# The norm's row: four broadcast matmuls of 128 columns in place of two of 256

## The chip, the cores and the metric

The kernel runs on one core of a Trainium2 chip. The metric is the device time of one execution in microseconds (us), the median of several runs. Each run of the profiler gives one more execution, with its own time.

## The reference, cut to what matters

A decoder trunk of two layers over 256 tokens of width 1024, in float32. Each layer is half an FFN, a mixer (attention and pooling in the even layer, spatial gating in the odd one) and another half FFN. Each of these six parts normalises its input first:

```python
def _rmsnorm(x, g):
    xf = x.astype(jnp.float32)
    y = xf * lax.rsqrt(jnp.mean(xf * xf, axis=-1, keepdims=True) + EPS)
    return (y * g.astype(jnp.float32)).astype(x.dtype)
...
    for layer in range(DEPTH):
        h = h + 0.5 * _swiglu(_rmsnorm(h, ffn_norm[layer, 0]), ffn_w_gate[layer, 0],
                              ffn_w_up[layer, 0], ffn_w_down[layer, 0])
        hn = _rmsnorm(h, mix_norm[layer])
        ...
```

The gain g is applied to the input of a projection; the factor rsqrt(...), one number for each token, is applied to the projection's output.

## The kernel before

The residual stream lies transposed in the chip's memory: 128 features on the partitions, eight such blocks, 256 tokens along the columns. Every weight arrives by DMA on SyncE's queue in chunks of up to 128 x 1024, is rounded by ScalarE into a high part (L169) and by VectorE into a low part (L177), and so each product of a weight and an activation is made of a few products of the type fp32r: mm2 (L216, L217) in the FFNs, with 256 and 512 columns, and mm3 (L210 to L212) in the mixers, with 256 to 512 columns. Products that aren't split have the type F32: the means of squares (L284, one column), the attention's values (L859 to L861, 64 columns), the mixing of the odd layer (L973, 128 columns), and the transposes (L563, L566, L793, L851, L874).

The order of the instructions on each engine is written out by hand (L107): it is the order of the calls in the program. The banks of the accumulator memory come in two sets of four, acc and rot.

The norm is worked in three steps. While the previous part ends, norm_hi, norm_lo and norm_sq (L264 to L279) make the scaled input x and the sums of squares. norm_sum (L281) multiplies them by a column of 1/1024 on TensorE, adds EPS on VectorE, takes the power -1/2 on GpSimd (L250), splits the result into a high and a low part, and writes, on GpSimd, each part times the identity into the tile diag (L295 to L298): four pieces of 128 x 128, high part first, left token half first. norm_row (L300) then multiplies a matrix of ones (ones_r, fp32r) by the low and the high diagonal. That puts each token's factor on all 128 partitions, as a row of 256 columns in the second half of a bank. ScalarE copies it to rb (L305), and in the FFNs VectorE copies half of it to rbh (L309).

norm_row runs six times, once in each part. In an FFN it is called in the second block of gate_up, before its third chunk, while norm_sum was called before its first one (L386); TensorE works on that block in between, and the epilogue of block 0, which multiplies by rb and rbh (L369, L371), follows at once. In the even mixer it stands behind the first two chunks of the pooling projection and right before the key and value products (L578, L623); in the odd mixer at the end of the first block of u (L994).

Of the kernel before, what the change touches and what calls it, by code (L numbers as in the profile page):

```python
# [16 lines left out]
P = 128  # L17
T = 256
TB = T // P
# [57 lines left out]
def trunk_kernel(  # L77
# [21 lines left out]
    nc = tc.nc  # L99
# [21 lines left out]
    def small(shape, tag, bufs=2):  # L121
        return spool.tile(shape, F32, tag=tag, name=nm(tag), bufs=bufs)
# [113 lines left out]
    ones_r = const.tile([P, P], F32R, name="ones_r")  # L236
# [19 lines left out]
    def norm_begin(gname, goff):  # L256
        s = Norm()
        s.gname, s.goff = gname, goff
        s.x = xpool.tile([P, KD, 2, T], F32R, tag="x", name=nm("x"), bufs=2)
        s.xl, s.xh = s.x[:, :, 0, :], s.x[:, :, 1, :]  # L260
        s.sum = None
        return s
# [36 lines left out]

    def norm_row(s, half=False):  # L300
        bc = s.bank[:, T : 2 * T]
        nc.tensor.matmul(bc, ones_r, s.dg[:, 1], start=True, stop=False, skip_group_check=True)
        nc.tensor.matmul(bc, ones_r, s.dg[:, 0], start=False, stop=True, skip_group_check=True)
        s.rb = small([P, T], "rb", bufs=2)
        nc.scalar.copy(s.rb, bc)  # L305
        if not half:
            return
        s.rbh = small([P, T], "rbh", bufs=2)
        nc.vector.tensor_scalar(s.rbh, bc, 0.5, None, op0=ALU.mult)  # L309
# [29 lines left out]
    def ffn(s, nxt_args, sets, first=False):  # L339
        with tc.tile_pool(name=nm("ffn"), bufs=2) as fp:  # L340
# [40 lines left out]
            def mid():  # L381
                norm_row(s, half=True)
                epilogue(0, gu0)
# [99 lines left out]
    def even_mixer(s, nxt_args):  # L483
        with tc.tile_pool(name="even", bufs=1) as ep:
# [91 lines left out]

            pool_in(0, turn_lat, 3)
            norm_row(s)  # L578
            advance(st["use"] + 4)
            nc.vector.tensor_mul(rqk, rqk, r1.unsqueeze(1).to_broadcast([P, 2, TB]))  # L580
# [329 lines left out]
    def odd_mixer(s, nxt_args):  # L910
        with tc.tile_pool(name="odd", bufs=1) as op:
# [78 lines left out]
            def gate_lo(c):  # L990
                cs = slice(2 * c, 2 * c + 2)
                nc.vector.tensor_sub(zl[:, cs, :], zs.pop(c), zh[:, cs, :].bitcast(F32))

            u_block(0, end=lambda: norm_row(s))  # L994
            for c in range(1, NG):
                def mid():
# [38 lines left out]
    s = norm_begin("ffn", 0)  # L1035
# [27 lines left out]
    s = ffn(s, ("mix", 0), (acc_bank, rot_bank), first=True)  # L1063
    s = even_mixer(s, ("ffn", KD))
    s = ffn(s, ("ffn", 2 * KD), (rot_bank, acc_bank))
    s = ffn(s, ("mix", KD), (acc_bank, rot_bank))
    s = odd_mixer(s, ("ffn", 3 * KD))
# [81 lines left out]
```

## Time and profile before

| | us |
|---|---|
| median of 3 runs | 909.33 (909.01 to 909.56) |
| profiled execution | 906.19 |
| its span, first to last instruction | 904.4 |
| TensorE's products (PE), busy | 894.2 |
| TensorE's weight loads (PEld), busy | 787.5 |
| VectorE (DVE), busy | 645.7 |
| ScalarE (ACT), busy | 496.1 |
| GpSimd (POOL), busy | 99.7 |

A product of TensorE has two records: the load of its 128 x 128 weights (PEld) and the product itself (PE). Their durations overlap, since both are pipelined and the ends of the products are modelled; what an instruction costs in a full stream is the time from its start to the start of the next one.

### The profile page before, as it was taken

To read this page: it belongs to the slowest core of one execution; us is meant where nothing else is said; L and a number is where in the kernel's file an instruction comes from. 1 tells how busy PE (TensorE), PEld (TensorE's weight loads), DVE (VectorE), ACT (ScalarE), POOL (GpSimd) and SP (SyncE) were. 2 spreads that over 40 slices of the span, in tenths; PEclk is the share of its full clock that TensorE was granted. 3 is DMA by queue.
4 is the path that set the end of the run, shared out by engine and by line. 5 is a ranking of instruction groups with operands and counts; after the bars stand their busy time and mean duration, and the time that the engine had idled before them with its cause. 6 is when DMAs were issued, how large, how long until landed. Compare 5 with 4: busy or idle time off the path is not lost.

```text
span 904.4 us, 13887 instructions
## 1 busy us (share of the span) xinstructions
PE 894.2 (99%) x5320; PEld 787.5 (87%) x5320; DVE 645.7 (71%) x973; ACT 496.1 (55%) x782; POOL 99.7 (11%) x130
## 2 busy tenths in 40 slices
PE   8999999999999999999999999999999999999998
PEld 6888888889898888888888888888899988888887
DVE  7787778658877877785558777756648668777652
ACT  7555554447575655564456555544545556555430
POOL 4200000016624000000030000000120220000000
PEclk9999999999999999999999999999999999999999
DMA  8565555635254555556644555575436455555750
GB/s 291 185 232 199 188 181 194 221 109 179 94 163 141 168 194 191 189 194 232 207 155 148 186 187 187 186 255 187 155 131 207 141 183 188 191 193 193 260 164 23
DMA packets 59281, 164.45 MB, mean 182 GB/s; under 512 B 5456, under 2 KB 7760, under 8 KB 59216
## 3 DMA queue, kind: packets, MB, share of 16 engines
q1 hardware_dynamic: 59216, 163.58, 54.0%
q8 instruction: 41, 0.67, 0.3%
q14 instruction: 24, 0.20, 0.1%
HBM read 162.51 MB, written 1.05 MB: 181 GB/s over the span
## 4 chain that ended last, share of the span: by engine, by line
PE 94%; DVE 2%; POOL 1%; issue 1%; ACT 1%; DMA 1%; SPq 0%; DVEq 0%; POOLq 0%
PE rot L217 27%; PE acc L217 26%; PE rot L216 13%; PE acc L216 13%; PE acc L211 3%; PE acc L210 3%; PE acc L212 2%; PE rot L210 1%; PE rot L211 1%; PE rot L212 1%; DMA raw<-w_gu 1%; PE rot L973 0%; POOL diag L297 0%; DVE wlo L182 0%; PE rot L821 0%
## 5 line engine op out<-in xcount | busy, mean ns | idle before, releaser
L177 DVE TENSOR_TENSOR wlo<-raw,whi 128x1024 fp32r<-128x1024 f32 (+2 forms) x298 | 353.1, 1228 | 76.3 <-ACT whi L169 76.2
L169 ACT CAST whi<-raw 128x1024 fp32r<-128x1024 f32 (+2 forms) x303 | 301.2, 1043 | 106.1 <-PE acc L217 39.8
L217 PE MATMUL acc<-x,whi 128*128 128x512 f32 x704 | 248.3, 397 | 0.0
L217 PE MATMUL rot<-x,whi 128*128 128x512 f32 x704 | 247.6, 396 | 0.0
L216 PE MATMUL acc<-x,wlo 128*128 128x256 f32 x704 | 197.7, 281 | 1.4 <-DVE wlo L182 1.4
L216 PE MATMUL rot<-x,wlo 128*128 128x256 f32 x704 | 196.6, 279 | 0.0
L217 PEld LDWEIGHTS acc<-x,whi 128*128 128x128 f32 x704 | 132.6, 188 | 31.3
L217 PEld LDWEIGHTS rot<-x,whi 128*128 128x128 f32 x704 | 132.2, 188 | 31.6
L216 PEld LDWEIGHTS acc<-x,wlo 128*128 128x128 f32 x704 | 133.1, 189 | 2.9 <-DVE wlo L182 2.9
L216 PEld LDWEIGHTS rot<-x,wlo 128*128 128x128 f32 x704 | 132.6, 188 | 0.0
L217 PE MATMUL rot<-pp,whi 128*128 128x512 f32 x352 | 123.4, 396 | 0.0
L217 PE MATMUL acc<-pp,whi 128*128 128x512 f32 x352 | 123.4, 396 | 0.0
L216 PE MATMUL acc<-pp,wlo 128*128 128x256 f32 x352 | 98.2, 279 | 0.0
L216 PE MATMUL rot<-pp,wlo 128*128 128x256 f32 x352 | 98.2, 279 | 0.0
L217 PEld LDWEIGHTS rot<-pp,whi 128*128 128x128 f32 x352 | 66.1, 188 | 15.9
L217 PEld LDWEIGHTS acc<-pp,whi 128*128 128x128 f32 x352 | 66.1, 188 | 15.9
L216 PEld LDWEIGHTS rot<-pp,wlo 128*128 128x128 f32 x352 | 66.3, 188 | 0.0
L216 PEld LDWEIGHTS acc<-pp,wlo 128*128 128x128 f32 x352 | 66.3, 188 | 0.0
L359 ACT COPY a<-rot 128x256 f32<-128x256 f32 x88 | 29.8, 373 | 55.5 <-PE rot L217 55.5
L359 ACT COPY a<-acc 128x256 f32<-128x256 f32 x88 | 29.8, 373 | 53.3 <-PE acc L217 53.3
L278 POOL TENSOR_TENSOR sqsum<-sq,sq 128x256 f32<-128x256 f32 x6 | 6.1, 1016 | 458.2 <-ACT sq L273 458.2
L361 DVE TENSOR_TENSOR gu<-rot,a 128x256 f32<-128x256 f32 x88 | 31.4, 419 | 34.1 <-ACT a L359 33.9
(246 smaller groups left out, 1037.4 us busy)
## 6 DMA issues: line engine op xcount, KB each, us to landing
raw<-w_gu SPq DMA_DIRECT2D x172, 512.0 KB, 4.6
raw<-w_down SPq DMA_DIRECT2D x88, 512.0 KB, 4.8
raw<-ew_out SPq DMA_DIRECT2D x8, 512.0 KB, 3.6
raw<-ow_v SPq DMA_DIRECT2D x8, 512.0 KB, 3.5
raw<-ow_u SPq DMA_DIRECT2D x8, 512.0 KB, 4.3
raw<-ow_out SPq DMA_DIRECT2D x8, 512.0 KB, 3.8
raw<-ew_p SPq DMA_DIRECT2D x4, 512.0 KB, 3.8
raw<-w_gu SPq DMA_DIRECT2D x7, 256.0 KB, 4.7
```

The lines of the kernel that those rows point to most:

```text
L169: nc.scalar.copy(hi[:, :n], r[:, :n])
L177: eng.tensor_sub(lo[:, :n], r[:, :n], hi[:, :n].bitcast(F32))
L210: nc.tensor.matmul(out, wl, xh, start=start, stop=False, skip_group_check=True)
L211: nc.tensor.matmul(out, wh, xl, start=False, stop=False, skip_group_check=True)
L212: nc.tensor.matmul(out, wh, xh, start=False, stop=stop, skip_group_check=True)
L216: nc.tensor.matmul(bank[:, 0:T], wl, x[:, 1, :], start=start, stop=False, skip_group_check=True)
L217: nc.tensor.matmul(bank, wh, x.rearrange("p s t -> p (s t)"), start=False, stop=stop, skip_group_check=True)
L278: nc.gpsimd.tensor_add(t, s.sum, sq)
L359: nc.scalar.copy(a[:, i, :], bank[:, 0:T])
L361: nc.vector.tensor_add(gu[:, i, :], bank[:, T:], a[:, i, :])
```

## The change

norm_row makes four products where it made two. The row of 256 columns is cut into two halves of 128 tokens; for each half the low diagonal and then the high one is multiplied by the same matrix of ones. Only the first of the four has `start=True`, and the high product of each half has `stop=True`. The sums are the same, and so is everything around.

```diff
     def norm_row(s, half=False):
         bc = s.bank[:, T : 2 * T]
-        nc.tensor.matmul(bc, ones_r, s.dg[:, 1], start=True, stop=False, skip_group_check=True)
-        nc.tensor.matmul(bc, ones_r, s.dg[:, 0], start=False, stop=True, skip_group_check=True)
+        for tb in range(TB):
+            ts = slice(tb * P, (tb + 1) * P)
+            nc.tensor.matmul(bc[:, ts], ones_r, s.dg[:, 1, ts], start=tb == 0, stop=False,
+                             skip_group_check=True)
+            nc.tensor.matmul(bc[:, ts], ones_r, s.dg[:, 0, ts], start=False, stop=True,
+                             skip_group_check=True)
         s.rb = small([P, T], "rb", bufs=2)
         nc.scalar.copy(s.rb, bc)
```

## Rows read from the trace of the kernel before

**Rows 1.** The busy time of the engines and the chain that ended last by engine (page), and the core's span with its mean granted TensorE clock.

```profile
PE 894.2 (99%) x5320; PEld 787.5 (87%) x5320; DVE 645.7 (71%) x973; ACT 496.1 (55%) x782; POOL 99.7 (11%) x130
PE 94%; DVE 2%; POOL 1%; issue 1%; ACT 1%; DMA 1%; SPq 0%; DVEq 0%; POOLq 0%
...
core 0: 904.4 us, clock 1.000
```

**Rows 2.** The two longest of ten lines of the waits of TensorE's products: who waited for whom, us in total, times, longest us.

```profile
PE acc L216 <- DVE wlo L182: 1.4, 4, 0.4
PE acc L302 <- POOL diag L297: 1.4, 1, 1.4
```

**Rows 3.** The instructions of L302: engine, operation, count, duration in ns (min/median/max), first and last start in us, shapes. PEldq is the queue of the weight loads.

```profile
L302 PEldq EVENT_SEMAPHORE  x5: 51/51/51, 211.5 to 730.8; - x5
L302 PE MATMUL acc<-diag,ones_r x4: 281/284/384, 27.8 to 672.3; 128*128 128x256 f32 x4
L302 PE MATMUL rot<-diag,ones_r x2: 279/280/280, 290.5 to 733.9; 128*128 128x256 f32 x2
```

**Rows 4.** The timeline of TensorE's products in the even mixer, the second and third FFN, the odd mixer and the fourth FFN: start in us, duration in us, engine, line, operation. L303's row, between the two of each pair, is left out.

```profile
213.59 0.28 PE L302 MATMUL acc<-diag,ones_r 128*128 128x256 f32 x1
...
213.83 0.39 PE L210 MATMUL acc<-whi,ckvl 128*128 128x512 f32 x1
...
290.51 0.28 PE L302 MATMUL rot<-diag,ones_r 128*128 128x256 f32 x1
...
290.74 0.28 PE L216 MATMUL acc<-x,wlo 128*128 128x256 f32 x1
...
474.46 0.28 PE L302 MATMUL acc<-diag,ones_r 128*128 128x256 f32 x1
...
474.69 0.28 PE L216 MATMUL rot<-x,wlo 128*128 128x256 f32 x1
...
672.30 0.28 PE L302 MATMUL acc<-diag,ones_r 128*128 128x256 f32 x1
...
672.54 0.28 PE L210 MATMUL acc<-x,wlo 128*128 128x256 f32 x1
...
733.89 0.28 PE L302 MATMUL rot<-diag,ones_r 128*128 128x256 f32 x1
...
734.13 0.29 PE L216 MATMUL acc<-x,wlo 128*128 128x256 f32 x1
```

**Rows 5.** The timeline of the first FFN around its norm_row, GpSimd (POOL), weight loads (PEld) and products (PE).

```profile
26.54 1.18 POOL L297 TENSOR_SCALAR diag<-cst_sb,r_lo 128x128 fp32r<-128x128 f32 x2
...
27.77 0.38 PE L302 MATMUL acc<-diag,ones_r 128*128 128x256 f32 x1 [1.41 <-POOL diag L297]
...
28.00 0.19 PEld L216 LDWEIGHTS rot<-x,wlo 128*128 128x128 f32 x1
...
28.00 0.28 PE L303 MATMUL acc<-diag,ones_r 128*128 128x256 f32 x1
28.11 0.28 PE L216 MATMUL rot<-x,wlo 128*128 128x256 f32 x1
```

**Rows 6.** The timeline of TensorE's products in the even mixer, where products of 512 columns are followed by products of 384.

```profile
216.37 0.39 PE L212 MATMUL acc<-whi,ckvh 128*128 128x512 f32 x1
216.60 0.33 PE L210 MATMUL rot<-whi,cql 128*128 128x384 f32 x1
216.77 0.34 PE L211 MATMUL rot<-wlo,cqh 128*128 128x384 f32 x1
```

**Rows 7.** The timeline of TensorE's products of few columns: the odd mixer (L973, 128 columns), the start of the fourth FFN (L284, one column), the even mixer (L860 and L861, 64 columns). A row with x8 stands for eight instructions in a row.

```profile
688.70 1.06 PE L973 MATMUL rot<-wt,v_sb 128*128 128x128 f32 x8
689.51 0.36 PE L210 MATMUL acc<-x,wlo 128*128 128x256 f32 x1
...
727.82 0.58 PE L284 MATMUL rot<-cmean,sqsum 128*128 128x1 f32 x4
728.26 0.36 PE L216 MATMUL acc<-x,wlo 128*128 128x256 f32 x1
...
242.14 0.39 PE L860 MATMUL rot<-v_sb,pT 128*128 128x64 f32 x2
242.36 0.39 PE L861 MATMUL rot<-v_sb,pT 128*128 128x64 f32 x2
242.58 0.28 PE L851 MATMUL rot<-cst_sb,sm 128*128 128x128 f32 x1
```

**Rows 8.** The weight loads grouped by line and shape: count, busy us, mean ns of one, idle before. The two remaining loads of L302 and of L303 write into a bank named rot.

```profile
L284 PEld LDWEIGHTS acc<-cmean,sqsum 128*128 128x128 f32 x16 | 2.2, 190 | 1.1 <-issue 1.0
L860 PEld LDWEIGHTS rot<-v_sb,pT 128*128 128x128 f32 x16 | 2.4, 192 | 0.0
...
L303 PEld LDWEIGHTS acc<-diag,ones_r 128*128 128x128 f32 x4 | 0.8, 190 | 0.0
L302 PEld LDWEIGHTS acc<-diag,ones_r 128*128 128x128 f32 x4 | 0.8, 189 | 1.8 <-POOL diag L297 1.7
...
L566 PEld LDWEIGHTS rot<-cst_sb,lat 128*128 128x128 f32 x4 | 0.5, 140 | 0.0
```

**Rows 9.** The instructions of L265 in the first 20 us and of L216 in the first 14 us: count, duration in ns (min/median/max), first and last start in us.

```profile
L265 ACT ACTIVATE x<-par_h x8: 492/496/508, 3.1 to 14.0; 128x256 fp32r<-128x256 f32 x8
...
L216 PE MATMUL acc<-x,wlo x20: 274/280/562, 4.7 to 13.6; 128*128 128x256 f32 x20
```

## The prediction, made before the changed kernel ran

> **What bounds the kernel now.** I read the page first. TensorE's products are recorded as busy for 99% of the span and its weight loads for 87%; no other engine passes 71%. The chain that ended last is 94% TensorE [rows 1]. So time added to TensorE's stream is time added to the run, unless it falls where TensorE waits anyway. The list of its waits is short: ten lines, of which the two longest are 1.4 us each; the second of these is a wait of the lines that change, for the diagonal at L302, once [rows 2]. The granted clock was 1.000 over the whole span [rows 1], the higher of the two levels (2.4 GHz), so rows from different stages can be compared.
>
> Next, the two lines themselves. norm_row runs six times; L302 stands there six times, each a product of 256 columns [rows 3], and L303 likewise; each has a weight load of its own, though all load the same ones_r [rows 8]. The start times in the timeline tell more than the durations, since the records overlap: from the start of L302 to the start of the product behind L303 it is 0.24 us in the even mixer, 0.23 in the second FFN, 0.23 in the third, 0.24 in the odd mixer, 0.24 in the fourth FFN [rows 4], 1.18 us for the five. The first FFN is different: there L302 comes after the wait, and from 27.77 to 28.11 the pair takes 0.34 us, 0.23 of it the first step [rows 5]. I count that as about 0.12 of start-up after a wait and two ordinary steps of 0.11.
>
> **What the change does to TensorE.** Twelve products of 256 columns become 24 of 128. The streamed columns stay the same (6 x 512); the weight loads double, from 12 to 24. What a 128-column product of this type costs is not in the trace: none with fp32r operands is narrower than 256 columns. I bound it.
>
> Lower end, streaming alone. A 512-column fp32r product takes 0.23 us from start to start and a 384-column one 0.17 [rows 6], a 256-column one 0.12 (half of the 0.24 of the pair) [rows 4]. That is 0.45 ns a column, proportional, so 128 columns would be 0.058 us, and four of them 0.232: as much as the pair takes now.
>
> Upper end, the price of a plain F32 product. In mix_block (L973) four F32 products of 128 columns are eight instructions, and the eight steps to the next product's start take 0.81 us, 0.10 each [rows 7]. With the 0.11 of the next paragraph, two of them make 0.222 us a product.
>
> Between them stands the weight load. Each product needs one, and the trace shows what a step is when the columns are too few to hide it. The mean products have a single column (L284): four instructions between 727.82 and 728.26, 0.11 us each. The value products have 64 columns (L860, L861): four between 242.14 and 242.58, again 0.11 [rows 7]. One column and 64 columns cost the same step, so the step there isn't streaming; it is the load. The fp32r loads of L302 and L303 have the same recorded duration as those (189 and 190 ns beside 190 to 192), while the loads of the transposes at L566 are shorter, 140 ns [rows 8]. The timeline of the first norm shows how a load lies: the load of the next product starts when the product before it starts (load of L216 at 28.00 beside L303 at 28.00) [rows 5]. A 256-column product of 0.12 us just covers a load of 0.11; one of 0.058 doesn't, and the load becomes the step. I take 0.111 us a product, the row nearest in kind (same load, fewer columns than 256), and keep 0.058 and 0.222 as the ends.
>
> The Trainium skill speaks for a price between the lower end and mine: "TensorE: Matmul & The Clock Gate", section "Back-to-back issue gap", puts a sustained stream of load and product pairs at about 81 ns for 128 columns. By that, as an estimate, the change would cost 0.4 us instead of my sum. No 128-column pair of this trace goes that fast: the steps at L973 are 0.10 [rows 7], so the trace does not agree.
>
> **The sum.** Five norms in a full stream: 4 x 0.111 = 0.444 each, 2.22 for the five, against 1.18 now: +1.04 us. All of it lies on the path, since TensorE doesn't wait there.
>
> The first norm waits for the diagonal, written in four pieces by GpSimd in the order high part left, high right, low left, low right. The two low pieces run from 26.54 to 27.72, so about 0.6 us each [rows 5]. Now L302 needs both low pieces. After the change the first two products need only the left pieces, about 0.6 us earlier; they fit into the wait, and two are left for after it: 0.12 + 2 x 0.111 = 0.34 us, as now, so nothing. That holds if a wait is set by the piece that is read. It is so elsewhere: the products of the first FFN read the tile x from 4.7 us on, while its last piece is written at 14.0 [rows 9]. If all four products waited for the last piece, it would be +0.22.
>
> Other engines: ScalarE's copy at L305 and then VectorE's L309 come 0.2 us later in each norm. Behind that copy ScalarE has the epilogue and the casts of the next weights (L169) queued, and TensorE needs both later; but none of the ten lines of its waits names L169, L177, L305, L309 or the epilogue, the longest being the split of the first chunks at L182 [rows 2], so the delay stays inside their slack. If that cover were gone, each norm would cost up to the same 0.2 us once more. In the even mixer the key and value products come right behind the pair [rows 4]; they and what hangs on them shift by the same 0.2 us, which is in the sum. No DMA and no GpSimd step is moved. A wait added in the middle of the four could show as a 51 ns semaphore instruction on TensorE's queue, as five of the six L302 have one [rows 3]; those before L302 cost no visible time, so I take nothing, and six times 0.051 = 0.31 us as the other end.
>
> Total +1.04 us: 906.19 us of the profiled execution becomes 907.23. The median of the runs, 909.33, stands 3.14 us above that execution; the same addition gives 910.37, rounded 910.4. With the two unkind ends (+0.22, +0.31) it is 910.9.
>
> **The rivals.**
> A narrow product is charged as plain F32 (slower). The fp32r rate would hold only for wide products, and at 128 columns each would cost 0.222 us. Five norms: 4 x 0.222 = 0.888, less 0.236 now, times five: +3.26. The first: 0.12 + 2 x 0.222 = 0.56 against 0.34, +0.22. Together +3.48, so 912.8. It decides as soon as a step is over about 0.15 us. For it: no fp32r product under 256 columns is there to deny it. Against: from 512 to 256 columns the cost falls in proportion, with no sign of a second price.
>
> The loads hide after all (no change). If a load of ones_r were as short as those of the transposes (some 50 ns less), or if a second load of the same weights cost nothing, streaming would set the step: 5 x 0.232 - 1.18 = -0.02, and in the first norm 0.12 + 2 x 0.058 = 0.24 against 0.34, -0.10. That gives 909.2. Against it: the records of these very loads are 189 ns, as long as those of the 0.11 us steps, and L303's load isn't shorter than L302's [rows 8]. The skill's 81 ns, named above, would land between, at an estimated 909.8.
>
> **How the numbers follow.** A measurement of this kernel tells about 0.2% from no change, 1.82 us: from 907.5 to 911.15 counts as the same. Load-bound step, 910.4 (up to 910.9): 0.70. F32 price, 912.8: 0.17. Hidden loads, 909.2: 0.10. Anything else, a shift of other waits in either direction: 0.03. So the same 0.80, slower 0.19, faster 0.01; a gain of 1.8 us has no place, as the only wait the change can shorten is 1.4 us long. The range goes from the hidden loads with the spread of the runs, 909.0, to the F32 price, 912.8.
>
> **What would show it.** In the profile of the changed kernel: 24 products of 128 columns and 24 loads under norm_row; from the first of the four to the product behind them 0.44 us in five norms (0.23 if loads hide, 0.89 at the F32 price); in the first norm two products at about 27.2 and two after 27.7, and the product behind them at 28.1. It would be wrong if the four were 0.44 us and the span didn't grow, which would mean that a later wait gave it back, or if the span grew by far more than the four steps, which would mean that something waits for the late row.

## The result and the profile after

The changed kernel takes 900.83 us (900.25 to 901.08, five runs). The ratio to the kernel before is 0.9913, 95% interval 0.9896 to 0.993: 0.9% faster, where no change was forecast and a gain of over 0.2% had been given a chance of 0.01. The five runs of the kernel before in that comparison stand at 909.01, 909.33, 909.47 and 909.56, and one at 906.12.

TensorE's products fill 99% of the span, as before; there are twelve products and twelve loads more. The first two lines of the page that answer to [rows 1]:

```profile
PE 888.1 (99%) x5332; PEld 789.8 (88%) x5332; DVE 644.9 (72%) x973; ACT 496.1 (55%) x782; POOL 99.6 (11%) x130
PE 94%; DVE 2%; POOL 1%; issue 1%; DMA 0%; ACT 0%; SPq 0%; DVEq 0%; POOLq 0%
```

L304 is the low product of the changed norm_row, L306 the high one. The instructions of L304 (answering to [rows 3]):

```profile
L304 PEldq EVENT_SEMAPHORE  x5: 51/51/51, 207.9 to 724.7; - x5
L304 PEld LDWEIGHTS acc<-diag,ones_r x8: 186/192/192, 26.8 to 666.1; 128*128 128x128 f32 x8
L304 PE MATMUL acc<-diag,ones_r x8: 223/275/328, 26.8 to 666.1; 128*128 128x128 f32 x8
L304 PE MATMUL rot<-diag,ones_r x4: 222/247/272, 286.9 to 728.0; 128*128 128x128 f32 x4
```

Twelve of L304 and twelve of L306, each of 128 columns, each with a load of some 190 ns: the change does what it says. The timeline of the products around norm_row in the second FFN (start and duration in us), to be held against [rows 4]:

```profile
286.64 0.39 PE L217 MATMUL acc<-x,whi 128*128 128x512 f32 x1
286.87 0.22 PE L304 MATMUL rot<-diag,ones_r 128*128 128x128 f32 x1
286.93 0.27 PE L306 MATMUL rot<-diag,ones_r 128*128 128x128 f32 x1
287.04 0.27 PE L304 MATMUL rot<-diag,ones_r 128*128 128x128 f32 x1
287.15 0.28 PE L306 MATMUL rot<-diag,ones_r 128*128 128x128 f32 x1
287.26 0.33 PE L216 MATMUL acc<-x,wlo 128*128 128x256 f32 x1
287.43 0.40 PE L217 MATMUL acc<-x,whi 128*128 128x512 f32 x1
```

From the first of the four to the product behind them it is 0.39 us, and the product behind them takes 0.17 to the next start in place of 0.12. So the four cost 0.56 - (0.23 + 0.12) = 0.21 us more than the pair, as forecast. The steps inside are 0.11 each, the step that was forecast from the loads; the first is 0.06, as the first load lies under the 512-column product before it (it starts at 286.64, shown further down), and what is saved there is paid in the step of the product behind. The first FFN, against [rows 5]:

```profile
26.78 0.33 PE L304 MATMUL acc<-diag,ones_r 128*128 128x128 f32 x1 [0.92 <-POOL diag L297]
26.95 0.28 PE L306 MATMUL acc<-diag,ones_r 128*128 128x128 f32 x1
27.36 0.33 PE L304 MATMUL acc<-diag,ones_r 128*128 128x128 f32 x1
27.53 0.27 PE L306 MATMUL acc<-diag,ones_r 128*128 128x128 f32 x1
27.64 0.33 PE L216 MATMUL rot<-x,wlo 128*128 128x256 f32 x1
```

Two products run inside the wait, the third starts 27.36 us in, and the next product of the stream starts 0.28 us after it. The piece-wise wait is there, and this norm costs next to nothing.

So the added work is what was forecast, and yet the span is 5.9 us shorter. The gain is in what wasn't touched. Here are the products of L217 alone (one in every step of the FFNs' stream, which is one product of 256 columns and one of 512) in a stretch of 100 us of each of the four FFNs. The columns are the stretch, its length, busy time of products and loads with their counts in brackets, the granted clock, the DMA share and GB/s. First the kernel before, then the changed one:

```profile
60.00:160.00 100.00, 100.00 (x284) 53.19 (x284) 1.00 0.57 191
310.00:410.00 100.00, 100.00 (x289) 54.01 (x289) 1.00 0.57 195
500.00:600.00 100.00, 100.00 (x284) 53.18 (x283) 1.00 0.59 200
760.00:860.00 100.00, 100.00 (x289) 54.02 (x289) 1.00 0.60 204
```

```profile
60.00:160.00 100.00, 100.00 (x290) 53.99 (x289) 1.00 0.60 202
310.00:410.00 100.00, 100.00 (x290) 53.90 (x289) 1.00 0.59 202
500.00:600.00 100.00, 100.00 (x290) 54.02 (x289) 1.00 0.59 201
760.00:860.00 100.00, 100.00 (x289) 53.89 (x289) 1.00 0.59 201
```

Before, the first and third FFN get through 284 steps in 100 us, the second and fourth through 289. After, all four get through 289 to 290. The clock is 1.00 in every row, no engine is waited for, and the instructions are the same. The start times give the pattern behind the counts. In the slow rhythm three steps repeat as 114, 232, 118, 240, 120, 236 ns, together 1060, so 353.3 a step of two products. The fast one repeats as 117, 230, 116, 230, 117, 230 or as 112, 233, 117, 231, 113 (or 118), 232, together 1040, so 346.7. The difference is 6.7 ns a step. From norm_row to the end of an FFN there are 304 steps of gate_up and 176 of the down projection, 480 in all: a slow FFN costs 480 x 6.7 ns = 3.2 us.

The same holds for the span. I counted the steps in the slow rhythm over the whole trace (three in a row that take over 1055 ns): 1032 before, 73 after. 959 x 6.7 ns is 6.4 us less; five norms at 0.21 us are 1.05 more, of which the even mixer gives 0.24 back at a later wait; 0.4 us are gained at the start, where the first transfers arrive. That makes 6.0 us, and the difference of 904.4 and 898.5 is 5.9.

One further run of the kernel before, in the first group of the experiments below, took 968.28 us at a granted clock of 0.851 and is left out.

### The profile page after: what moved, and what is told of

It is laid out like the page before. It is cut to its first block, busy times and chain, and to the rows that moved or that the text cites. A ratio compares the mean times of both kernels' runs of the same rounds, so it can differ in the third digit from the quotient of the medians.

```text
span 898.5 us, 13906 instructions
## 1 busy us (share of the span) xinstructions
PE 888.1 (99%) x5332; PEld 789.8 (88%) x5332; DVE 644.9 (72%) x973; ACT 496.1 (55%) x782; POOL 99.6 (11%) x130
## 3 DMA queue, kind: packets, MB, share of 16 engines
HBM read 162.51 MB, written 1.05 MB: 182 GB/s over the span
## 4 chain that ended last, share of the span: by engine, by line
PE 94%; DVE 2%; POOL 1%; issue 1%; DMA 0%; ACT 0%; SPq 0%; DVEq 0%; POOLq 0%
PE rot L217 26%; PE acc L217 26%; PE rot L216 14%; PE acc L216 14%; PE acc L211 2%; PE acc L210 2%; PE acc L212 2%; PE rot L210 1%; PE rot L212 1%; PE rot L211 1%; DMA raw<-w_gu 0%; DVE sA L603 0%; PE rot L977 0%; POOL diag L297 0%; DVE wlo L177 0%
## 5 line engine op out<-in xcount | busy, mean ns | idle before, releaser
L177 DVE TENSOR_TENSOR wlo<-raw,whi 128x1024 fp32r<-128x1024 f32 (+2 forms) x298 | 353.0, 1228 | 74.7 <-ACT whi L169 74.6
L217 PE MATMUL rot<-x,whi 128*128 128x512 f32 x704 | 245.7, 392 | 0.0
L217 PE MATMUL acc<-x,whi 128*128 128x512 f32 x704 | 245.5, 391 | 0.0
L216 PE MATMUL acc<-x,wlo 128*128 128x256 f32 x704 | 197.9, 281 | 2.2 <-DVE wlo L182 2.2
L216 PE MATMUL rot<-x,wlo 128*128 128x256 f32 x704 | 197.5, 280 | 0.0
L217 PEld LDWEIGHTS rot<-x,whi 128*128 128x128 f32 x704 | 131.7, 187 | 29.1
L217 PEld LDWEIGHTS acc<-x,whi 128*128 128x128 f32 x704 | 131.7, 187 | 28.5
L216 PEld LDWEIGHTS acc<-x,wlo 128*128 128x128 f32 x704 | 133.0, 189 | 3.4 <-DVE wlo L182 3.3
L216 PEld LDWEIGHTS rot<-x,wlo 128*128 128x128 f32 x704 | 133.1, 189 | 0.0
L217 PE MATMUL rot<-pp,whi 128*128 128x512 f32 x352 | 122.2, 391 | 0.0
L217 PE MATMUL acc<-pp,whi 128*128 128x512 f32 x352 | 122.2, 391 | 0.0
L216 PE MATMUL rot<-pp,wlo 128*128 128x256 f32 x352 | 98.6, 280 | 0.0
L216 PE MATMUL acc<-pp,wlo 128*128 128x256 f32 x352 | 98.6, 280 | 0.0
L217 PEld LDWEIGHTS rot<-pp,whi 128*128 128x128 f32 x352 | 65.8, 187 | 14.4
L217 PEld LDWEIGHTS acc<-pp,whi 128*128 128x128 f32 x352 | 65.8, 187 | 14.4
L216 PEld LDWEIGHTS rot<-pp,wlo 128*128 128x128 f32 x352 | 66.5, 189 | 0.0
L216 PEld LDWEIGHTS acc<-pp,wlo 128*128 128x128 f32 x352 | 66.5, 189 | 0.0
L374 ACT ACTIVATE gu<-gu 128x512 f32<-128x512 f32 x44 | 27.8, 633 | 50.5 <-DVE gu L373 50.5
```

Of the source, the lines that this page charges most:

```text
L177: eng.tensor_sub(lo[:, :n], r[:, :n], hi[:, :n].bitcast(F32))
L216: nc.tensor.matmul(bank[:, 0:T], wl, x[:, 1, :], start=start, stop=False, skip_group_check=True)
L217: nc.tensor.matmul(bank, wh, x.rearrange("p s t -> p (s t)"), start=False, stop=stop, skip_group_check=True)
L374: nc.scalar.activation(t, t, AF.Silu)
```

## The experiments

The kernel before was run again beside every group of experiments, and its time isn't one number. Its 114 runs stand in steps of 3.2 us. I read them as the count of its slow FFNs; the one profile of this kernel bears that out, with two slow FFNs at 906.19:

| group of runs | median | no slow FFN (899.4 to 899.9) | one (902.5 to 903.6) | two (905.4 to 907.0) | three (909.0 to 910.0) | four (912.4 to 913.3) |
|---|---|---|---|---|---|---|
| comparison with the change | 909.33 | 0 | 0 | 1 | 4 | 0 |
| first four experiments | 903.45 | 0 | 15 | 11 | 1 | 1 |
| next four | 912.48 | 0 | 0 | 2 | 12 | 15 |
| next four | 906.22 | 2 | 6 | 15 | 8 | 0 |
| last three | 909.38 | 0 | 0 | 8 | 8 | 5 |

So a ratio to it depends on the group, and below I read the steps and the profiles, not the ratios. The four groups of experiments ran on chips 3, 3, 14 and 12 by number; the two on chip 3 differ the most, so the chip alone isn't the reason.

**The four narrow products in the FFNs alone, and in the mixers alone.** Do one part alone.

```diff
+        if half:        # first kernel; "if not half" in the second
+            ...         # the four products of the change
+        else:
+            ...         # the pair
```

> Two theories from the comparison of the traces. Rhythm: the FFN's stream (one product of 256 columns, one of 512, repeated) runs at 0.347 or at 0.353 us a step of two, keeps its rhythm until something interrupts it, and four narrow products right ahead of it leave it in the fast one, while the wide pair leaves it to chance. Place: the gain comes from six times two more instructions as such (count, code place, waits), wherever they stand. Here only the four FFNs have the four narrow products, the two mixers keep the pair. Rhythm: all of the gain, 900.0 to 901.0 us, all four FFNs at 0.347. Place: a part of the gain, since a third of the instructions is gone: 902 to 905.

> The other half: narrow products in the two mixers alone. Rhythm: no gain, some FFNs at 0.353 as before, 909.3 (or 906.2 where one FFN fewer is slow) plus up to 0.4 us for the added steps. Place: a third of the gain or more, 904 to 907, with FFNs at 0.347.

Measured: FFNs alone 900.60 us, ten of eleven runs between 900.3 and 901.5 and one at 903.67; mixers alone 906.52, in the steps of the kernel before (903.3 to 912.7). The gain sits in the FFNs, and the 0.4 us of the mixers can't be seen. Place falls.

**Four wide products.** The same count, none narrow.

```diff
+        for last in (False, True):
             nc.tensor.matmul(bc, ones_r, s.dg[:, 1], start=True, ...)
             nc.tensor.matmul(bc, ones_r, s.dg[:, 0], start=False, stop=True, ...)
```

> Four products of 256 columns in each norm_row: the pair is made twice, the second time with the start mark again, so the count is that of the changed kernel and no product is narrow. Rhythm: no product is bound by its load, so the rhythm stays a matter of chance and some FFNs run at 0.353; 0.24 us more in six places, 907 to 911. Place: the count is the same as after the change, so about 901 to 902.

Measured: 901.00 us, ten of twelve runs between 900.6 and 901.3, two at 904.2 and 904.5. All four FFNs of its profile are fast:

```profile
60.00:160.00 100.00, 100.00 (x290) 53.94 (x289) 1.00 0.59 199
310.00:410.00 100.00, 100.00 (x290) 54.08 (x289) 1.00 0.60 201
500.00:600.00 100.00, 100.00 (x290) 54.00 (x289) 1.00 0.59 201
760.00:860.00 100.00, 100.00 (x289) 54.03 (x289) 1.00 0.60 200
```

The narrow width isn't what makes the FFNs fast; the theory as I had put it falls on that point. Place had said 901 to 902 here too, but it had fallen on the mixers.

**Four narrow products, then the pair.**

```diff
+        for tb in range(TB):
+            ...         # the four products of the change
         nc.tensor.matmul(bc, ones_r, s.dg[:, 1], start=True, ...)
         nc.tensor.matmul(bc, ones_r, s.dg[:, 0], start=False, stop=True, ...)
```

> Four narrow products first and then the wide pair (which starts the sum anew, so the row is the same). Rhythm, if what stands last ahead of the stream decides: the pair disturbs it again, some FFNs at 0.353, 2.7 us more work in the six norms, 908 to 912. If narrow products anywhere close by are enough: all FFNs at 0.347 and 902 to 903.

Measured: 914.86 us (914.5 to 915.3), the slowest of all and with hardly any spread. All four FFNs are slow:

```profile
60.00:160.00 100.00, 100.00 (x284) 53.18 (x284) 1.00 0.58 195
310.00:410.00 100.00, 100.00 (x284) 53.19 (x284) 1.00 0.56 190
500.00:600.00 100.00, 100.00 (x284) 53.18 (x283) 1.00 0.56 187
760.00:860.00 100.00, 100.00 (x284) 53.18 (x283) 1.00 0.57 188
```

The four narrow products are there, and the gain is not only gone but turned round. What stands right ahead of the stream picks its rhythm, and it can do so the same way in every run.

**Other orders.** Four narrow products behind the pair (in the FFNs, into another bank); three products, the wide one last or first.

```diff
+                burst(sets[0]())      # 4 x (ones_r times ones_r, 128 columns), behind norm_row
```

```diff
-        nc.tensor.matmul(bc, ones_r, s.dg[:, 0], ...)
+        for tb in range(TB):          # high part narrow; in the other kernel the low part
+            nc.tensor.matmul(bc[:, ts], ones_r, s.dg[:, 0, ts], ...)
```

> The four runs so far leave this: the FFN's stream has two fast rhythms (0.3467 us a step of two) and a slow one (0.3533), and what comes right ahead of it picks one; four narrow or four wide products led to fast ones, the pair to slow or fast, four narrow and then the pair always to slow. Here norm_row keeps its pair, and in the FFNs four more narrow products (ones times ones, into a bank that nobody reads) follow directly. Theory Last: only the last few products count, so four narrow ones behind the pair give fast in all FFNs; 900.5 to 902 us, the added steps being 4 x 0.44. Theory Count: the number of products put between decides, four is good and two or six are bad; then all FFNs are slow here, as with four narrow and the pair: about 914.

> Three products: two narrow for the low part, then one wide for the high part. Theory Last: a wide product stands last, as in the pair, so slow FFNs, three or four of them: 909 to 913. Theory Count: three is new, nothing is said beyond that it is one rhythm in every FFN that isn't held up by GpSimd.

> Three products: one wide for the low part, then two narrow for the high part. Theory Last: narrow ones stand last, so fast FFNs, 899.8 to 901, a shade under the changed kernel since one load-bound step is missing in each norm. Theory Count: as for the other order of three, the same rhythm as there.

Measured: pair and four narrow 911.35, three runs near 908.0, five around 911 and four near 914.5, so two to four slow FFNs; Last and Count both fall. Wide last: 910.55 (909.7 to 914.6). Wide first: 900.28 (900.1 to 901.1), five of five with no slow FFN. The width of the last product isn't a rule by itself.

**The pair, called one chunk later.**

```diff
-  {0: lambda: norm_sum(s, bank), 2: mid}
+  {0: lambda: norm_sum(s, bank), 3: mid}
```

> The kernel before, with norm_row of the FFNs called one chunk later (before the fourth chunk of block 1), so that the diagonal is ready well ahead and the pair is never held up by GpSimd, not by a few nanoseconds either. Theory Hold: the pair, met by an undisturbed fast stream, always leads to the slow rhythm (step pattern 117, 230, 118, 233, 118, 241 behind it), and the fast FFNs of the kernel before come from those few nanoseconds; then FFNs 2 to 4 are slow in every run, and the first as well, whose wait of 1.4 us is gone: 911 to 913 us, with little spread. Rival: the draw is made by something else (the place in memory, the state of the chip), so the times stay mixed between 902.7 and 909.4, less up to 1.4 us for the wait.

Measured: 911.85, in two groups, five runs at 908.9 to 910.0 and seven at 911.8 to 912.7; the profile, of the first group, has FFNs 2 to 4 slow and the first fast. This is the picture of Hold with the first FFN left to chance, which I had thought settled as well. The later place brought waits of its own (two of 0.2 us for the low weights of L177 in the blocks behind), so it isn't a clean edit.

**Four narrow products in the down projection.** Is the rhythm tied to norm_row?

```diff
+                    if hf == 0 and b == 4:
+                        burst(sets[0]())
```

> norm_row keeps its pair; four narrow products (ones times ones, into a bank that nobody reads) stand in each FFN's down projection instead, behind its fifth chunk, where the stream is undisturbed. Theory Draw: the rhythm belongs to the stream of products alone and is drawn anew at any interruption, and four narrow ones out of an undisturbed stream of either rhythm lead to fast; so an FFN that is slow up to there is fast behind it: 136 steps of two by 6.7 ns, 0.9 us back for each slow FFN, against 4 x 0.44 us for the added products. With three slow FFNs 908.6, with four 910.9. Rival Stage: the rhythm comes from the stage (its tiles, its banks, the other engines' work), and nothing changes inside an FFN: 911.3 with three, 914.5 with four.

Measured: 907.78 (904.5 to 912.5). L217 in the second, third and fourth FFN, each in a stretch ahead of the four products and one behind:

```profile
310.00:400.00 90.00, 90.00 (x261) 48.63 (x260) 1.00 0.57 194
410.00:460.00 50.00, 49.59 (x141) 26.34 (x141) 1.00 0.57 193
480.00:590.00 110.00, 110.00 (x318) 59.44 (x317) 1.00 0.56 185
600.00:635.00 35.00, 35.00 (x101) 18.62 (x100) 1.00 0.59 188
740.00:840.00 100.00, 100.00 (x289) 54.02 (x289) 1.00 0.56 194
855.00:890.00 35.00, 35.00 (x100) 18.61 (x100) 1.00 0.45 143
```

Ahead of them 261 products in 90 us, 318 in 110 and 289 in 100, all the fast rhythm (345 to 346 ns a step); behind them 141 in 49.6 us of work and 100 in the last 35, the slow one (350 to 352). The 101 in 35 of the third FFN are too few to tell by count; their start times repeat as 113, 233, 117, 241, 120, 236 ns, the slow rhythm too. So the rhythm changes inside an FFN, at an interruption, against the rival; but here the four narrow products turned three fast FFNs slow, and the first FFN, slow ahead of them, stayed slow: Draw falls as well in what it said of four narrow ones. They are not good in themselves. The fast rhythm they met was that of 112, 233 ns; at norm_row, after the changed kernel's mean products, it is the one of 117, 230 or the slow one.

**The changed kernel again, and two versions meant to be better.**

```diff
+        if half:
+            ...         # one wide low product, two narrow high ones
+        else:
+            ...         # the pair
-  {0: lambda: norm_sum(s, bank), 2: mid}      # first of the two only
+  {0: lambda: norm_sum(s, bank), 3: mid}
```

> The changed kernel once more, beside the kernel before in the same stretch of chip time, since the kernel before has stood at 903.5 and at 912.5 us in the two calls so far, in steps of 3.2 us that count its slow FFNs. Theory Draw: the changed kernel draws fast nearly always, whatever the kernel before does: 900.2 to 901.1 in nine runs of ten, the rest 3.2 us higher. Rival: the draw is common to both (a state of the chip), and the changed kernel goes up with the kernel before.

> A version meant to beat both: in the FFNs one wide and two narrow products, called one chunk later so that the first norm needn't wait for the diagonal; the mixers keep the pair. Theory Draw: fast in all FFNs if the draw of one wide and two narrow doesn't hang on the hold by GpSimd: 898.8 to 899.8, some 1 us from the first norm's wait. If that draw needed the hold, slow FFNs in steps of 3.2 us: 903 to 912.

> The same without the later call: one wide and two narrow products in the FFNs, the pair in the mixers, norm_row where it was. Theory Draw: fast in all FFNs, 900.0 to 900.6, within 0.3 us of the version with three products everywhere, since the mixers give a part of the added steps back at a later wait. Rival Place (the two mixers matter): 902 or more.

Measured: the changed kernel 900.84 (seven of eight runs at 900.4 to 901.0, one at 903.72), ratio 0.9934 (0.9912 to 0.9956), while the kernel before stood at 906.22. The two others fail: 905.00 (902.9 to 909.6) and 907.19 (900.8 to 910.4). One wide and two narrow products, all fast in five runs above, came out with up to three slow FFNs here. The version above had them in the mixers as well, where these two have the pair, and it ran on another chip; which of this made the difference isn't shown. In the later-called one the first FFN is slow from norm_row on; FFNs 2 to 4 are fast right behind it, and TensorE then waits 0.3 us for a low weight of L177, behind which two of them go on slowly.

**What the hold does.** In the kernel before the first load of the pair is held by GpSimd. The timeline of its second FFN: the two low pieces of the diagonal end at 289.14 + 1.19 = 290.33, and the load of L302 starts 0.05 us later, 0.11 after the product ahead of it started, while a load that nothing holds starts with that product. The last two rows are those of the third FFN:

```profile
289.14 1.19 POOL L297 TENSOR_SCALAR diag<-cst_sb,r_lo 128x128 fp32r<-128x128 f32 x2
...
290.27 0.39 PE L217 MATMUL acc<-x,whi 128*128 128x512 f32 x1
290.38 0.19 PEld L302 LDWEIGHTS rot<-diag,ones_r 128*128 128x128 f32 x1
...
474.23 0.39 PE L217 MATMUL rot<-x,whi 128*128 128x512 f32 x1
474.32 0.19 PEld L302 LDWEIGHTS acc<-diag,ones_r 128*128 128x128 f32 x1
```

The delay lies under the 512-column product and so shows in no list of waits. In nanoseconds the load of L302 comes 107, 96 and 110 after that product in FFNs 2 to 4 of this trace. The 96 went with the slow rhythm, the others with the fast one. Over all profiles with the pair, where the fast rhythm came in: 96 ns, slow in three of three; 100 to 110, fast in five of five; 2 to 3 ns, unheld (the later call), slow in two of two. In the changed kernel the first product needs only the third piece and its load starts at once (compare 286.64 in the timeline above):

```profile
286.64 0.19 PEld L304 LDWEIGHTS rot<-diag,ones_r 128*128 128x128 f32 x1
```

Three edits of GpSimd's order test it: with the pair, with one wide and two narrow products in all six norms, and with the change's four.

```diff
-        for i, part in enumerate((rh.bitcast(F32), rl)):
+        for i, part in ((1, rl), (0, rh.bitcast(F32))):   # pair; and one wide, two narrow
             for tb in range(TB):
```

```diff
-        for i, part in enumerate((rh.bitcast(F32), rl)):
-            for tb in range(TB):
+        for tb in (1, 0):                                 # with the change's four products
+            for i, part in enumerate((rh.bitcast(F32), rl)):
```

> The kernel before with one edit on GpSimd: the two low pieces of the diagonal are written first. Then the first load of the pair, which needs only low pieces, is not held by GpSimd in FFNs 2 to 4 (in the traces so far it starts 96 to 110 ns late there, and 96 went with the slow rhythm, 100 to 110 with the fast one). Theory Hold: without the hold the pair always meets an undisturbed stream and leads to the slow rhythm in FFNs 2 to 4; only the first FFN, whose wait remains, is left to chance: 909.0 to 912.9 in every run, nothing below. Rival Chance: the hold doesn't matter, and times are spread as those of the kernel before, 899.5 to 913 with most at 903 to 910.

> The changed kernel with one edit on GpSimd: the pieces of the left token half are written last, so that the first narrow product needs the last piece and its load is held as that of the old pair was (in the changed kernel it starts 2 to 3 ns after the product before, unheld). Theory Hold: the changed kernel is fast because its first load isn't held; held, the draw is open again, and slow FFNs come back in some runs, steps of 3.2 us over 900.7, a spread of at least 3 us. Rival Four: four narrow products lead to fast from any entry, 900.2 to 901.1 as before.

> One wide and two narrow products in all six norms, with the low pieces written first, so that the wide low product isn't held. Where it was held, FFNs came out slow or fast; where it wasn't (the later call), three of three were fast right behind it. Theory Hold: FFNs 2 to 4 fast in every run, the first left to chance: 899.8 to 900.8, some runs 3.2 us more. Rival Chance: slow FFNs in any number, up to 910.

Measured, the pair without the hold: 912.47, ten of twelve runs at 912.2 to 913.0 with four slow FFNs, one at 909.23 and one at 906.37, which is below what I had allowed; of the kernel before beside it five of 21 runs had four slow ones. Product and load start together (290.10), and every FFN is slow:

```profile
290.10 0.39 PE L217 MATMUL acc<-x,whi 128*128 128x512 f32 x1
290.10 0.19 PEld L302 LDWEIGHTS rot<-diag,ones_r 128*128 128x128 f32 x1
```

```profile
60.00:160.00 100.00, 100.00 (x284) 53.18 (x284) 1.00 0.57 193
310.00:410.00 100.00, 100.00 (x284) 53.19 (x284) 1.00 0.56 188
500.00:600.00 100.00, 100.00 (x285) 53.18 (x284) 1.00 0.58 196
760.00:860.00 100.00, 100.00 (x284) 53.19 (x284) 1.00 0.58 195
```

The four narrow products with the hold: 904.02, eight of ten runs at 903.7 to 904.3, one slow FFN, two at 900.8. In the second FFN the load comes 0.10 us after the product, and that FFN is slow; in the fourth it comes as late, and that one is fast:

```profile
287.14 0.39 PE L217 MATMUL acc<-x,whi 128*128 128x512 f32 x1
287.24 0.19 PEld L304 LDWEIGHTS rot<-diag,ones_r 128*128 128x128 f32 x1
```

```profile
60.00:160.00 100.00, 100.00 (x289) 53.92 (x289) 1.00 0.60 199
310.00:410.00 100.00, 100.00 (x284) 53.18 (x283) 1.00 0.58 194
500.00:600.00 100.00, 100.00 (x289) 53.94 (x289) 1.00 0.60 206
760.00:860.00 100.00, 100.00 (x290) 53.91 (x289) 1.00 0.60 202
```

One wide and two narrow without the hold: 900.38 (899.9 to 900.9), six of six with no slow FFN, ratio 0.9904 (0.9875 to 0.9934). The same six norms with the hold had given 900.28, also with no slow FFN (in that profile the loads of FFNs 2 and 3 come 95 and 83 ns late), so these runs alone don't speak for the hold; 907.19 came from the version with the pair in the mixers. This version stands level with the changed kernel, at one product and some 0.1 us a norm less.

## Why the prediction was wrong

**Right.** TensorE is the bound; the change makes 24 products and 24 loads; the step of a narrow product is 0.11 us, that of the rows bound by their loads, not the 0.06 of streaming nor the 0.22 of plain F32; a norm in a full stream costs 0.21 us more (0.205, 0.213 and 0.215 in the second FFN, the odd mixer and the fourth FFN, by the shift of the products behind); the first norm's wait is by pieces, and it costs nothing. Both rivals are refuted by the same steps. The 81 ns that the Trainium skill gives for 128 columns ("TensorE: Matmul & The Clock Gate", section "Back-to-back issue gap") aren't met either: no step inside the four is under 0.108 us but the first. The late row of ScalarE and VectorE made nobody wait.

**A shade off.** The even mixer gave its 0.21 us back at a later wait, which the sum had counted in full: 0.84 us in five norms in place of 1.04.

**Wrong.** The step that failed is "All of it lies on the path", with what it takes for granted: that the stream behind norm_row runs at the same pace whatever stands ahead of it, so that the change is worth its own instructions and no more. And so "a gain of 1.8 us has no place" was wrong: the place is the stream behind norm_row in the four FFNs, 480 steps of two products in each. The runs showed that this stream has rhythms of 346.7 and 353.3 ns a step, keeps the one it has until an interruption, and that norm_row is such an interruption, worth 3.2 us for each FFN. The kernel before had two slow FFNs in its profile and mostly three in the runs of the first comparison; the change left none: 3 x 3.2 us less 0.84 is 8.8, against 8.5 measured. The prediction priced what a norm costs and had no term for what it does to the stream behind it. The trace of before held a sign of that, 284 and 289 products in equal stretches of equal work. So did the 3.14 us between the profiled execution and the median, about one slow FFN, which the prediction carried along as a constant while it took 1.82 us for the limit of what can be told apart. I took steps at a hundredth of a microsecond from a few rows of each stage, where 0.353 and 0.347 are both 0.35.

**Why the change draws fast, and the pair mixed.** Shown for FFNs 2 to 4: the products of norm_row and the hold of its first load by GpSimd, hidden from the list of waits, decide together. Where that load isn't held (it starts within 5 ns of the product ahead), the profiles show one outcome for each sequence right behind norm_row, whichever rhythm came in: the pair slow in six of six entries, the change's four products fast in nine of nine, one wide and two narrow fast in seven of seven, two narrow and one wide slow in three of three, four narrow and the pair slow in three of three. Where it is held, the pair goes to either side within some 10 ns; the change's four go slow at 101 ns and fast at 100 and 16, one wide and two narrow slow at 107 and 23 and fast at 95, 83 and 14; only the four wide ones are fast in all three.

The change does two things at once, then. It makes four products, and it moves the first one off the last diagonal piece. Four products with the hold stand at 904.02 where the kernel before beside them has 909.38; without it they come to 900.84 in another group; and without the hold the pair is slower, 912.47. So neither alone is the whole gain. That the products are narrow isn't needed, and their 0.84 us are no part of it. Only argued: that the share of slow FFNs in the kernel before differs from group to group because GpSimd's time against TensorE's differs by those nanoseconds.

**Open.** Why the stream has these rhythms, and why one sequence of products leads to one of them, is not settled: four wide and four narrow products lead to fast and three with the wide one last to slow, and four narrow ones in the down projection, not held either, led to slow in four of four. The runs give no rule that foretells a new sequence. The first FFN, which enters after a wait of a microsecond, remained a matter of chance in several versions.

## What to carry to other kernels

On a stream of products that bounds the kernel, count the products in equal stretches of equal work before summing an edit by its own instructions: here a difference of 2% between stages with the same code was a rhythm, and an edit ahead of the stream switched it. Run the kernel before often enough to see whether its times stand in steps, and don't credit an edit's own instructions with a step that a reordering on another engine moves as well. Look for holds at the start of the weight loads, not only in the list of waits.

## What the runs showed of the hardware that was not expected

The same stream of fp32r products of 256 and 512 columns, at the granted clock 1.00, runs at 346.7 or 353.3 ns a step and keeps its rhythm over 160 us. A delay of 107 ns in place of 96 in one hidden weight load went with 3.2 us over the FFN behind it. A narrow fp32r product in a run of such costs 0.11 us, as much as an F32 product of one column [rows 7], and a run of them pushes its last load onto the product behind, whose step grows from 0.12 to 0.17.
